# A gated linear recurrence beside dense products: emission of the recurrence's steps moved by one or two products

## The chip, the cores and the metric

The kernel runs on one core of one Trainium2 chip. The metric is the device time of one execution in microseconds (us); the time before is 2263.52 us, the median of three runs (2262.01 to 2264.18). The core has a matrix engine (PE, whose weight loads PEld run beside it), a vector engine (DVE), a scalar engine (ACT), GpSimd (POOL) and SyncE (SP), which starts the DMAs. Each engine works through its own queue of instructions; semaphores tie the queues together.

## The reference

Two transformer blocks follow each other on 1024 tokens of width 1024, all in float32. The change touches the first mixer of the first block only:

```
proj = h @ w_in                       # 1024 x 4096: q, f, i, g
k    = (1 - lb) * sigmoid(-f);  decay = lb + (1 - lb) * sigmoid(f)
q    = silu(q) * 128 ** -0.5
S_t  = diag(decay_t) S_{t-1} + k_t v_t^T ;  o_t = S_t^T q_t     # 8 heads of 128
out  = (rms_norm per head of o) * out_norm * silu(g) @ w_out
```

With one layer the lower bound lb is 0. After this mixer come a squared-ReLU MLP, a second mixer (a short convolution beside a retention) and a second MLP, which the change leaves as they are.

## The kernel before, in words

Every large product is made of three float32r matmuls (high by high, high by low, low by high part), which the helper `mm3` (L210) issues. This text calls one such triple over 512 columns "a product". `unit` (L216) makes one 128x512 tile of a projection from 8 products; `unit_b` (L230) makes the values' tiles from triples of 256 columns, half a product each. Between them a small planner runs: `at(delay, fn)` (L144) files a function under a slot number, and `tick` (L147) runs all functions filed under the present slot, in the order in which they were filed, and raises the number. `unit` ticks after its fourth product and at its end, `unit_b` after each 8 triples of 256 columns, so there are four products' worth of columns between two ticks. What a function issues in a tick goes to the end of each engine's queue, and the queue is worked through in that order.

In `run`, the first mixer goes through 8 heads. For each head a `unit` pair makes f (4 ticks) and a pair makes q (4 ticks); before each even head but the first, `unit_b` makes the values of two heads (8 ticks). After q's first half (L792 to L795) DVE multiplies the tile by the row norm (L609), ACT takes the sigmoid (L794) and DVE forms the query tile qf (L795); the same follows for the second half. Then `hgrn_scan` (L354) files the recurrence of the head under later slots, by the table `SCAN_AT` (L37), counted from the slot of the call:

- `diag` at 0: 64 small matmuls (L367), and DVE copies them under a mask (L372)
- `level0` at 0: nine DVE instructions (queries and totals, L386 to L434)
- `level1` at 2: 64 small matmuls (`scores`, L413); on DVE the queries forward (L401 to L403), new queries (L389, L390, behind copies by ACT at L388), the keys (L442, L443), the masked copies (L420) and totals (L432 to L434)
- `level2` at 5: `scores` again (L413), then DVE L402, L403, L442, L443, L420
- `level(16)`, `level(32)`, `level(64)` at 7, 8, 10: small matmuls (L367 for 16 tokens, L485 for 32 and 64), a copy by DVE (L476) or ACT (L489), then three DVE instructions: totals (L492), keys kr (L493), queries qf (L494)
- `krt` at 12: seven transposes of kr on PE (L539)
- `states` at 15: L554 on PE, L560 and L562 on DVE; `outs` at 16: L574 and L576 on PE, squares on ACT (L585), sums on DVE (L586); `scale` at 21 (L593); `final` at 24 (L603)

Two heads take 24 slots: 8 for the values, 4 each for f, q, f and q. If the even head of a pair calls at slot 16, the odd one calls at slot 24, 8 slots later. So two heads' steps meet in some slots. Slot 24 holds the previous odd head's `final`, the even head's `level(32)`, the odd head's `diag` and `level0`. Slot 26 holds the even head's `level(64)`, then the odd head's `level1`; slot 28 the even head's `krt`. Slot 16 holds `final` of the head two before, `outs` of the one before, and `diag` and `level0` of the head itself. After head 7 the gates' units take the place of the values; their tiles are handled by `gate` (L612), which files a DVE product (L620) for the next tick and another (L624) for the one after it.

Of the kernel before, what the change touches and what calls it, by code (L numbers as in the profile page):

```python
# [17 lines left out]
MUL, ADD, SUB, MAX = ALU.mult, ALU.add, ALU.subtract, ALU.max  # L18
# [3 lines left out]
T = 1024  # L22
D = 1024
KT = 8
HALF = 512
# [9 lines left out]


SCAN_AT = (0, 0, 2, 5, 7, 8, 10, 12, 15, 16, 21, 24)  # L37
RETENTION_AT = (2, 4, 5, 5, 13, 14)
CONV_NORM_AT = (2, 4, 5)
CONV_SPLIT_AT = (50, 52, 54, 56)  # L40
# [57 lines left out]
class Kernel:  # L98
    def __init__(self, tc, ctx, x, w, consts, masks, tab, out):
        self.tc, self.nc = tc, tc.nc  # L100
        self.low = self.nc.vector
        self.x_dram, self.w_dram, self.c_dram = x, w, consts
        self.m_dram, self.tab_dram, self.out_dram = masks, tab, out
        cp = ctx.enter_context(tc.tile_pool(name="consts", bufs=1))
        self.cp = cp
        self.sm = ctx.enter_context(tc.tile_pool(name="small", bufs=2))
        self.tp = ctx.enter_context(tc.tile_pool(name="tmp", bufs=N_TMP))
        self.slots = Slots(ctx.enter_context(tc.tile_pool(name="slots", bufs=1)), N_SLOTS)
        self.acc = ctx.enter_context(tc.tile_pool(name="acc", bufs=4, space=bass.MemoryType.PSUM))
        self.ps2 = ctx.enter_context(tc.tile_pool(name="ps2", bufs=4, space=bass.MemoryType.PSUM))  # L110
        self.slot = 0
        self.plan = defaultdict(list)
        self.n = 0
        self.stage = {}
        self.split = {}
        self.next_load = 0
        self.next_split = 0
        self.next_use = 0
        self.look = N_LOOK
        self.apart = 0  # L120
        self.limit = FIRST_MLP
        self.dram = ctx.enter_context(tc.tile_pool(name="dram", bufs=1, space=bass.MemoryType.DRAM))
# [22 lines left out]
        self.plan[self.slot + delay].append(fn)  # L145

    def tick(self):  # L147
        while self.slot in self.plan:
            for fn in self.plan.pop(self.slot):
                fn()  # L150
        self.slot += 1

    def drain(self):
        while self.plan:
            self.tick()


# [52 lines left out]
    def mm3(self, ps, ah, al, bh, bl, start, stop):  # L210
        mm = self.nc.tensor.matmul
        mm(ps, lhsT=ah, rhs=bh, start=start, stop=False)  # L212
        mm(ps, lhsT=ah, rhs=bl, start=False, stop=False)  # L213
        mm(ps, lhsT=al, rhs=bh, start=False, stop=stop)  # L214

    def unit(self, w, src, half):  # L216

# [136 lines left out]
    def hgrn_scan(self, h, qf, kr, f, v):  # L354
# [6 lines left out]
        st = {"off": 0}  # L361
# [8 lines left out]
        def diag():  # L370
            ps = small(self.bank(), lambda t: qf[:, t:t + 32], 32)
            ve.copy_predicated(ac, self.masks[:, M_DIAG:M_N], ps)  # L372
            st["tots"] = S.get("tots")

# [15 lines left out]
        def advance(i, half, tot):  # L392
            b = B4[i]
            n = HALF // (4 * b)
            r = st.pop((i, half))
            rv = r[:, :768].rearrange("p (v n b) -> p v n b", v=6, b=b)
            g = slice(half * n, (half + 1) * n)
            qv = qf.rearrange("p (n j b) -> p j n b", j=4, b=b)[:, :, g]
            d0 = tot.rearrange("p (n j) -> p j n", j=4)[:, 0:1, g, None].to_broadcast([P, 2, n, b])
            if i == 0:  # L400
                ve.tensor_tensor(qv[:, 0], qv[:, 0], d0[:, 0], op=MUL)  # L401
            ve.tensor_tensor(qv[:, 1], rv[:, 0], d0[:, 0], op=MUL)  # L402
            ve.tensor_tensor(qv[:, 2:4], rv[:, 3::2], d0, op=MUL)  # L403
            S.put(r)

        def scores(i):
            b = B4[i]
# [37 lines left out]


        def level0():
            for half in range(2):
                queries(0, half, f)
            st["d1"], st["e0"] = totals(0, f)  # L450

        def level1():
            keep = scores(0)
            for half in range(2):
                advance(0, half, f)
                queries(1, half, st["d1"])
            keys(0, f, st["e0"])
            keep()
            st["tot"], st["e1"] = totals(1, st["d1"])
            S.put(f)  # L460

        def level2():
            keep = scores(1)
            for half in range(2):
                advance(1, half, st["d1"])
            keys(1, st["d1"], st["e1"])
            keep()

        def level(b):
            n = T // (2 * b)  # L470
            ps = self.bank()
            qv = qf.rearrange("p (n two b) -> p n two b", two=2, b=b)
            kv = kr.rearrange("p (n two b) -> p n two b", two=2, b=b)
            if b == 16:
                pv = small(ps, lambda t: qv[:, t // (2 * b):(t + 32) // (2 * b), 1, :], 16)
                ve.copy_predicated(ac.rearrange("p (n two b) -> p n two b", two=2, b=b)[:, :, 1, :],  # L476
                                   self.masks[:, M_16:M_DIAG].rearrange("p (n b) -> p n b", b=b),
                                   pv.rearrange("p (n b) -> p n b", b=b))
            else:
                av = a.rearrange("p (n two b) -> p n two b", two=2, b=b)  # L480
                nb = P // (2 * b)
                for c in range(NCH):
                    for j in range(nb):
                        r = slice(2 * b * j, 2 * b * j + b)
                        mm(ps[r, c * b:(c + 1) * b], lhsT=kv[:, c * nb + j, 0, :], rhs=qv[:, c * nb + j, 1, :],  # L485
                           start=True, stop=True)
                for j in range(nb):
                    r = slice(2 * b * j, 2 * b * j + b)
                    nc.scalar.copy(av[r, j::nb, 1, :], ps[r, :NCH * b].rearrange("p (n b) -> p n b", b=b))  # L489
            tv = st["tot"].rearrange("p (n two) -> p n two", two=2)  # L490
            new = st["tots"][:, st["off"]:st["off"] + n]
            ve.tensor_tensor(new, tv[:, :, 0], tv[:, :, 1], op=MUL)  # L492
            nc.vector.tensor_tensor(kv[:, :, 0, :], kv[:, :, 0, :], tv[:, :, 1:2].to_broadcast([P, n, b]), op=MUL)  # L493
            nc.vector.tensor_tensor(qv[:, :, 1, :], qv[:, :, 1, :], tv[:, :, 0:1].to_broadcast([P, n, b]), op=MUL)  # L494
            st["off"] += n
            st["tot"] = new
            if b == 16:
                for r in range(0, P, 32):
                    nc.scalar.copy(a3[r:r + 32, :, r:r + 32], ac[r:r + 32].rearrange("p (c t) -> p c t", t=32))
# [22 lines left out]
            S.put(st["os"])  # L522

        t = SCAN_AT
        for i, fn in enumerate((diag, level0, level1, level2)):
            self.at(t[i], fn)
        for i in range(3):
            self.at(t[4 + i], lambda i=i: level(16 << i))
        for i, fn in enumerate((krt, states, outs, scale, final)):
            self.at(t[7 + i], fn)  # L530

    def transpose7(self, src, dst, scale):

# [108 lines left out]
    def run(self):  # L642
# [126 lines left out]
        for h in range(8):  # L769
            if h % 2 == 0 and h:  # L770
                vs = [S.get("v"), S.get("v")]
                ws = self.use(2)
                for p in range(4):
                    ps = self.unit_b(ws, u, p)
                    self.values(ps, p, vs, zs)
                self.done(ws)
            f, kr, qf = S.get("f"), S.get("kr"), S.get("qf")
            ws = self.use()
            for half in range(2):
                tk = slice(half * HALF, (half + 1) * HALF)  # L780
                ps = self.unit(ws[0], u, half)
                z = self.times_rb(ps, half)
                nc.scalar.activation(f[:, tk], z, AF.Sigmoid)
                nc.scalar.activation(kr[:, tk], z, AF.Sigmoid, scale=-1.0)
                nc.scalar.activation(f[:, tk], f[:, tk], AF.Identity, scale=self.omlb[:, h:h + 1],
                                     bias=self.lb[:, h:h + 1])
            self.done(ws)
            ws = self.use()
            for half in range(2):
                tk = slice(half * HALF, (half + 1) * HALF)  # L790
                ps = self.unit(ws[0], u, half)
                z = self.times_rb(ps, half)  # L792
                sg = self.tmp()
                nc.scalar.activation(sg, z, AF.Sigmoid)  # L794
                nc.vector.scalar_tensor_tensor(qf[:, tk], z, self.c1[:, h:h + 1], sg, op0=MUL, op1=MUL)  # L795
                if half == 1:
                    self.hgrn_scan(h, qf, kr, f, vs[h % 2])
            self.done(ws)

# [969 lines left out]
```

## Time and profile before

| | |
|---|---|
| time, median of 3 runs | 2263.52 us (2262.01 to 2264.18) |
| profiled execution, its own time | 2263.14 us |
| span of its instructions | 2261.4 us |
| PE busy | 2233.7 us, 99% of the span |
| DVE busy | 1775.9 us, 79% |
| ACT busy | 856.0 us, 38% |
| mean granted clock of PE | 0.997 |
| PE busy from 100 to 200, 200 to 300, 300 to 400 us (first mixer) | 97.39, 97.39, 97.27 us |
| PE busy in each 100 us from 600 to 1100 us | 100.00 us |

Times are microseconds from the start of the span. "Busy" is the time in which an engine works on an instruction; a number in brackets behind a row, as [1.01 <-DVE qf L795], is the idle time of the engine just before that instruction and the instruction on the other engine that ended it. [...]

### The profile page before, as it was taken

Reading aid. Unit: us, or ns where it says so; the run is one execution under the profiler, and the core shown is the slowest. Engines: PE = TensorE matmul, PEld = TensorE weight load, DVE = VectorE, ACT = ScalarE, POOL = GpSimd, SP = SyncE. Lnnn points to the kernel's source line nnn. Section 1 sums busy time; section 2 is a strip of 40 time slices with the busy share of each in tenths; the row PEclk is TensorE's granted clock in tenths of the full one; section 3 lists DMA queues with packets and bytes.
Section 4 is the critical chain, followed back from the end, with each engine's and each line's share of the span. In section 5 each row is a group of like instructions: output and inputs, shape, how many; then the busy total and the mean of one; then the engine's idle time right before and its main releaser. Section 6 shows DMA issues by size and latency. Waiting matters only on the chain.

```text
span 2261.4 us, 32861 instructions
## 1 busy us (share of the span) xinstructions
PE 2233.7 (99%) x13102; PEld 1883.5 (83%) x13102; DVE 1775.9 (79%) x2674; ACT 856.0 (38%) x1259; POOL 347.0 (15%) x340
## 2 busy tenths in 40 slices
PE   8999999999999999999999999999999999999998
PEld 7888897888888888888889888888888888888887
DVE  6757668736988888989996556885798888889896
ACT  6333333434433335433344232224533333634322
POOL 0020101101111111222210011000111111222223
PEclk9999999999999999999999999999999999999999
DMA  5001011122344448544514101113334445744442
GB/s 182 30 29 39 20 39 39 47 85 112 128 175 157 153 167 291 167 140 160 194 38 187 38 29 46 39 38 118 125 135 177 149 151 212 263 142 155 153 158 75
DMA packets 82521, 270.30 MB, mean 120 GB/s; under 512 B 9152, under 2 KB 11712, under 8 KB 82368
## 3 DMA queue, kind: packets, MB, share of 16 engines
q1 hardware_dynamic: 81792, 267.67, 33.8%
q8 instruction: 103, 1.69, 0.3%
q10 hardware_dynamic: 576, 0.52, 0.1%
q14 instruction: 50, 0.41, 0.1%
HBM read 190.57 MB, written 77.59 MB: 119 GB/s over the span
## 4 chain that ended last, share of the span: by engine, by line
PE 89%; DVE 8%; ACT 2%; issue 1%; DMA 0%; SPq 0%; DVEq 0%; ACTq 0%
PE acc L212 21%; PE acc L213 21%; PE acc L214 21%; PE ps L212 7%; PE ps L213 7%; PE ps L214 7%; PE ps L574 1%; PE ps L576 1%; PE ps L554 1%; DVE ac L420 1%; DVE lo L178 1%; DVE tmp L609 1%; DVE r L389 0%; PE ps L485 0%; PE ps L539 0%
## 5 line engine op out<-in xcount | busy, mean ns | idle before, releaser
L212 PE MATMUL acc<-hi,hi 128*128 128x512 f32 (+1 forms) x824 | 315.1, 382 | 0.5 <-ACT acc L1255 0.4
L214 PE MATMUL acc<-hi,lo 128*128 128x512 f32 (+1 forms) x824 | 313.8, 381 | 0.0
L213 PE MATMUL acc<-lo,hi 128*128 128x512 f32 (+1 forms) x824 | 313.8, 381 | 0.0
L212 PE MATMUL acc<-uh,hi 128*128 128x512 f32 x768 | 305.6, 398 | 0.0
L214 PE MATMUL acc<-uh,lo 128*128 128x512 f32 x768 | 299.4, 390 | 0.0
L213 PE MATMUL acc<-ul,hi 128*128 128x512 f32 x768 | 299.1, 389 | 0.0
L212 PE MATMUL ps<-hi,hi 128*128 128x512 f32 x712 | 277.2, 389 | 0.0
L214 PE MATMUL ps<-hi,lo 128*128 128x512 f32 x712 | 277.0, 389 | 0.0
L213 PE MATMUL ps<-lo,hi 128*128 128x512 f32 x712 | 277.0, 389 | 0.0
L1198 ACT ACTIVATE hq<-hq 128x512 f32<-128x512 f32 x128 | 81.0, 634 | 333.3 <-DVE hq L1197 267.3
L212 PEld LDWEIGHTS acc<-hi,hi 128*128 128x128 f32 x824 | 154.9, 188 | 31.4 <-ACT acc L1255 1.1
L214 PEld LDWEIGHTS acc<-hi,lo 128*128 128x128 f32 x824 | 154.9, 188 | 29.8
L213 PEld LDWEIGHTS acc<-lo,hi 128*128 128x128 f32 x824 | 154.9, 188 | 29.7 <-issue 0.2
L214 PEld LDWEIGHTS acc<-uh,lo 128*128 128x128 f32 x768 | 144.1, 188 | 30.8
L212 PEld LDWEIGHTS acc<-uh,hi 128*128 128x128 f32 x768 | 144.2, 188 | 30.0 <-ACT v L638 0.2
L213 PEld LDWEIGHTS acc<-ul,hi 128*128 128x128 f32 x768 | 144.3, 188 | 28.7 <-issue 0.5
L214 PEld LDWEIGHTS ps<-hi,lo 128*128 128x128 f32 x712 | 133.6, 188 | 28.0
L212 PEld LDWEIGHTS ps<-hi,hi 128*128 128x128 f32 x712 | 133.6, 188 | 27.7
L213 PEld LDWEIGHTS ps<-lo,hi 128*128 128x128 f32 x712 | 133.7, 188 | 27.6
L189 ACT CAST hi<-h 128x1024 fp32r<-128x1024 f32 x96 | 100.4, 1055 | 134.0 <-DVE lo L190 76.5
L190 DVE TENSOR_TENSOR lo<-h,hi 128x1024 fp32r<-128x1024 f32 x96 | 122.1, 1280 | 6.3 <-ACT hi L189 6.3
L178 DVE TENSOR_TENSOR lo<-w,hi 128x1024 fp32r<-128x1024 f32 x74 | 89.8, 1219 | 28.4 <-ACT hi L175 28.3
(278 smaller groups left out, 4644.3 us busy)
## 6 DMA issues: line engine op xcount, KB each, us to landing
w<-in_w SPq DMA_DIRECT2D x202, 512.0 KB, 4.5
hf<-f SPq DMA_DIRECT2D x28, 512.0 KB, 2.6
hfull<-hq SPq DMA_DIRECT2D x28, 512.0 KB, 3.5
hg<-g SPq DMA_DIRECT2D x28, 512.0 KB, 4.1
h<-hfull SPq DMA_DIRECT2D x28, 512.0 KB, 3.6
h<-hf SPq DMA_DIRECT2D x28, 512.0 KB, 4.4
h<-hg SPq DMA_DIRECT2D x28, 512.0 KB, 3.4
xs<-x SPq DMA_DIRECT2D x16, 512.0 KB, 2.8
```

Of the source, the lines that this page charges most:

```text
L178: self.low.tensor_tensor(lo, st, hi.bitcast(F32), op=SUB)
L189: self.nc.scalar.copy(hi, src)
L190: self.low.tensor_tensor(lo, src, hi.bitcast(F32), op=SUB)
L212: mm(ps, lhsT=ah, rhs=bh, start=start, stop=False)
L213: mm(ps, lhsT=ah, rhs=bl, start=False, stop=False)
L214: mm(ps, lhsT=al, rhs=bh, start=False, stop=stop)
L420: ve.copy_predicated(av[:, j:], mask[:, v0:v1], pm[:, v0:v1])
L554: nc.tensor.matmul(ps[:, c * P:(c + 1) * P], lhsT=kt[:, t], rhs=v[:, t], start=True, stop=True)
L574: nc.tensor.matmul(o, lhsT=a3[:, i, :], rhs=v[:, t], start=True, stop=(i == 0))
L576: nc.tensor.matmul(o, lhsT=qx[:, t], rhs=s[:, t], start=False, stop=True)
L609: self.nc.vector.tensor_tensor(z, ps, self.rb[:, half * HALF:(half + 1) * HALF], op=MUL)
L1198: nc.scalar.activation(t, t, AF.Square)
```

## The change

No instruction of the computation is added or taken out; the order in which they stand in the engines' queues changes. `mm3` counts the products issued (`work`), and a new function `defer(n, fn)` puts a function on a list that is looked through after each triple: it runs once n products more have been issued, at the next tick at the latest. A table beside `SCAN_AT` says which step is deferred within its slot, and by how many products: `diag` by 2, `level0`, `level(32)`, `level(64)` and `outs` by 1, the others by 0. In `level2` the queries are moved forward first, and the rest (scores, keys, copies) is deferred by 2. In `level(16)` the small matmuls stay at the tick, and the masked copy and the three DVE instructions behind it are deferred by 1. The product L795 of q's first half is filed for the next tick; before that of the second half, everything on the list is issued first.

```diff
+SCAN_LATE = (2, 1, 0, 0, 0, 1, 1, 0, 0, 1, 0, 0)
     def tick(self):
+        self.flush()
         while self.slot in self.plan:
...
+    def defer(self, n, fn):
+        self.late.append((self.work + n, fn))
+        self.late.sort(key=lambda e: e[0])
+    def flush(self, upto=float("inf")):
+        while self.late and self.late[0][0] <= upto:
+            self.late.pop(0)[1]()
...
         mm(ps, lhsT=al, rhs=bh, start=False, stop=stop)
+        self.work += bh.shape[-1] / HALF
+        self.flush(self.work)
...
         def level2():
-            keep = scores(1)
             for half in range(2):
                 advance(1, half, st["d1"])
-            keys(1, st["d1"], st["e1"])
-            keep()
+            def rest():
+                keep = scores(1)
+                for half in range(2):
+                    S.put(st.pop((1, half)))
+                keys(1, st["d1"], st["e1"])
+                keep()
+            self.defer(2, rest)
...
             if b == 16:
                 pv = small(ps, lambda t: qv[:, t // (2 * b):(t + 32) // (2 * b), 1, :], 16)
-                ve.copy_predicated(ac.rearrange("p (n two b) -> p n two b", two=2, b=b)[:, :, 1, :],
-                                   self.masks[:, M_16:M_DIAG].rearrange("p (n b) -> p n b", b=b),
-                                   pv.rearrange("p (n b) -> p n b", b=b))
+                self.defer(1, lambda: (ve.copy_predicated(
+                    ac.rearrange("p (n two b) -> p n two b", two=2, b=b)[:, :, 1, :],
+                    self.masks[:, M_16:M_DIAG].rearrange("p (n b) -> p n b", b=b),
+                    pv.rearrange("p (n b) -> p n b", b=b)), next_level(b, qv, kv)))
             else:
...
+                next_level(b, qv, kv)
+        def next_level(b, qv, kv):
+            n = T // (2 * b)
             tv = st["tot"].rearrange("p (n two) -> p n two", two=2)
             new = st["tots"][:, st["off"]:st["off"] + n]
             ve.tensor_tensor(new, tv[:, :, 0], tv[:, :, 1], op=MUL)
...
+        steps = (diag, level0, level1, level2, *(lambda i=i: level(16 << i) for i in range(3)),
+                 krt, states, outs, scale, final)
+        for i, (fn, n) in enumerate(zip(steps, SCAN_LATE)):
+            self.at(t[i], (lambda fn=fn, n=n: self.defer(n, fn)) if n else fn)
...
-                nc.vector.scalar_tensor_tensor(qf[:, tk], z, self.c1[:, h:h + 1], sg, op0=MUL, op1=MUL)
-                if half == 1:
+                def product(tk=tk, z=z, sg=sg, qf=qf, h=h):
+                    nc.vector.scalar_tensor_tensor(qf[:, tk], z, self.c1[:, h:h + 1], sg, op0=MUL, op1=MUL)
+                if half == 0:
+                    self.at(0, product)
+                else:
+                    self.flush()
+                    product()
                     self.hgrn_scan(h, qf, kr, f, vs[h % 2])
```

Of the tiles, `tots` is taken in `level0` in place of `diag`, and the tiles r are given back in `level1` and in the deferred part of `level2`.

## Rows read from the trace of the kernel before

**Rows 1.** From the profile's page: busy time of PE over the span (time, share, instructions), and the chain of work that ended last, its shares by engine. From the table by stretches, one stretch in which PE only makes products: length, PE busy time (and matmuls), PEld, DVE, ACT and POOL busy time, granted clock, DMA share, GB/s.

```profile
PE 2233.7 (99%) x13102; PEld 1883.5 (83%) x13102; DVE 1775.9 (79%) x2674; ACT 856.0 (38%) x1259; POOL 347.0 (15%) x340
...
PE 89%; DVE 8%; ACT 2%; issue 1%; DMA 0%; SPq 0%; DVEq 0%; ACTq 0%
...
700.00:800.00 100.00, 100.00 (x443) 82.81 (x442) 84.01 (x113) 33.94 (x48) 15.87 (x11) 1.00 0.41 149
```

**Rows 2.** What PE waited for from 60 to 470 us, the stretch of the recurrences: total us, times, longest us. These are all the rows of that answer.

```profile
PE ps L485 <- DVE qf L494: 4.1, 5, 1.0
PE ps L367 <- DVE qf L795: 4.0, 4, 1.0
PE ps L413 <- DVE kr L443: 1.8, 3, 0.6
PE ps L576 <- DVE s L560: 0.6, 1, 0.6
```

**Rows 3.** PE in order of time around the meeting of heads 2 and 3, the second of the four pairs: start, length, line, tile and count, and in brackets the idle time before. L413 is `level2` of head 2, L485 with 128x32 `level(32)` of head 2, L367 `diag` of head 3, L485 with 128x64 `level(64)` of head 2, L413 after it `level1` of head 3, L539 `krt` of head 2.

```profile
170.64 0.89 PE L413 MATMUL ps<-r,kr 128*32 128x48 f32 x64 [0.61 <-DVE kr L443]
...
182.86 0.64 PE L485 MATMUL ps<-qf,kr 128*32 128x32 f32 x29 [0.90 <-DVE qf L494]
...
184.82 0.46 PE L367 MATMUL ps<-qf,kr 128*32 128x32 f32 x32 [1.01 <-DVE qf L795]
...
192.64 1.15 PE L485 MATMUL ps<-qf,kr 128*64 128x64 f32 x16
193.71 0.89 PE L413 MATMUL ps<-r,kr 128*32 128x48 f32 x64
...
200.39 0.93 PE L539 MATMUL ps<-cs,kr 128*128 128x128 f32 x7
```

**Rows 4.** DVE in order of time in the same pair, up to the meeting: the sums behind `outs`, the keys of `level1` of head 2, the query products of both halves, the queries of `level(16)`, and the second half's eviction (L609).

```profile
155.16 0.69 DVE L586 TENSOR_REDUCE ss<-tmp 128x4 f32<-128x512 f32 x1 [1.10 <-ACT tmp L585]
...
169.89 0.60 DVE L443 TENSOR_TENSOR kr<-kr,f 128x256 f32<-128x256 f32 x1
...
180.46 0.75 DVE L795 SCALAR_TENSOR_TENSOR qf<-tmp,c,tmp 128x512 f32<-128x512 f32 x1 [0.70 <-ACT tmp L794]
...
182.03 0.69 DVE L494 TENSOR_TENSOR qf<-qf,tots 128x512 f32<-128x512 f32 x1
182.63 0.69 DVE L609 TENSOR_TENSOR tmp<-acc,rb 128x512 f32<-128x512 f32 x1
184.01 0.75 DVE L795 SCALAR_TENSOR_TENSOR qf<-tmp,c,tmp 128x512 f32<-128x512 f32 x1 [0.70 <-ACT tmp L794]
```

**Rows 5.** DVE in order of time behind the meeting: the masked copy of `diag`, the first instruction of `level0`, a weight split (L178), the keys of `level(64)` of head 2, the first instruction of `level1` of head 3, and the first behind the last one of `level1`.

```profile
185.97 0.44 DVE L372 COPY_PREDICATED ac<-masks,ps 128x256 f32<-128x256 uint8 x1
186.31 0.86 DVE L386 TENSOR_TENSOR r<-qf,f 128x384 f32<-128x384 f32 x1
...
191.88 1.22 DVE L178 TENSOR_TENSOR lo<-w,hi 128x1024 fp32r<-128x1024 f32 x1
193.02 0.16 DVE L492 TENSOR_TENSOR tots<-tots 128x8 f32<-128x8 f32 x1
193.82 0.69 DVE L493 TENSOR_TENSOR kr<-kr,tots 128x512 f32<-128x512 f32 x1 [0.64 <-PE ps L485]
...
195.03 0.38 DVE L401 TENSOR_TENSOR qf<-qf,f 128x128 f32<-128x128 f32 x1
...
204.00 0.28 DVE L402 TENSOR_TENSOR qf<-r,tots 128x128 f32<-128x128 f32 x1
```

**Rows 6.** PE in the other pairs, in order of time: `level(32)` and `krt` of the first pair; `level2` and `krt` of the third; `level2` and `krt` of the fourth; and `level(32)` of head 7.

```profile
88.82 0.64 PE L485 MATMUL ps<-qf,kr 128*32 128x32 f32 x29 [0.60 <-DVE qf L494]
...
104.86 0.93 PE L539 MATMUL ps<-cs,kr 128*128 128x128 f32 x7
...
266.17 0.89 PE L413 MATMUL ps<-r,kr 128*32 128x48 f32 x64 [0.61 <-DVE kr L443]
...
294.44 0.93 PE L539 MATMUL ps<-cs,kr 128*128 128x128 f32 x7
...
360.24 0.89 PE L413 MATMUL ps<-r,kr 128*32 128x48 f32 x64 [0.62 <-DVE kr L443]
...
387.98 0.93 PE L539 MATMUL ps<-cs,kr 128*128 128x128 f32 x7
...
408.24 0.70 PE L485 MATMUL ps<-qf,kr 128*32 128x32 f32 x32 [0.67 <-DVE qf L494]
```

**Rows 7.** The granted clock, from the table by stretches for PE alone: length, PE busy time (matmuls), granted clock, DMA share, GB/s. The first two stretches are in the second pair, the third at the same place in the third pair.

```profile
184.00:186.00 2.00, 1.18 (x37) 0.91 0.03 8
186.00:188.00 2.00, 2.00 (x11) 0.50 0.00 0
...
280.00:282.00 2.00, 1.65 (x42) 1.00 0.00 0
```

**Rows 8.** Three rows for durations. Two triples of the values apart on PE (start to start of the first matmul of two neighbouring triples of 256 columns), and the gate's DVE product behind `level1` of head 7.

```profile
190.03 0.28 PE L212 MATMUL acc<-hi,uh 128*128 128x256 f32 x1
...
190.39 0.28 PE L212 MATMUL acc<-hi,uh 128*128 128x256 f32 x1
...
393.39 0.68 DVE L620 TENSOR_TENSOR tmp<-tmp,on 128x512 f32<-128x512 f32 x1
```

More of the change, by code (lines that the diff above doesn't have):

```diff
@@ L112, in __init__ @@
         self.plan = defaultdict(list)
+        self.late = []
+        self.work = 0.0
         self.n = 0
@@ L151, in tick @@
         self.slot += 1
+    def defer(self, n, fn):
[4 more added lines that the diff above has]
+            self.late.pop(0)[1]()
     def drain(self):
-        while self.plan:
+        while self.plan or self.late:
             self.tick()
@@ L372, in diag @@
             ve.copy_predicated(ac, self.masks[:, M_DIAG:M_N], ps)
-            st["tots"] = S.get("tots")
         def queries(i, half, tot):
@@ L394, in advance @@
             n = HALF // (4 * b)
-            r = st.pop((i, half))
+            r = st[i, half]
             rv = r[:, :768].rearrange("p (v n b) -> p v n b", v=6, b=b)
@@ L403, in advance @@
             ve.tensor_tensor(qv[:, 2:4], rv[:, 3::2], d0, op=MUL)
-            S.put(r)
         def scores(i):
@@ L447, in level0 @@
         def level0():
+            st["tots"] = S.get("tots")
             for half in range(2):
@@ L455, in level1 @@
                 advance(0, half, f)
+                S.put(st.pop((0, half)))
                 queries(1, half, st["d1"])
@@ L524, in hgrn_scan @@
         t = SCAN_AT
[L525 to L530, printed above, removed]
+        steps = (diag, level0, level1, level2, *(lambda i=i: level(16 << i) for i in range(3)),
+                 krt, states, outs, scale, final)
+        for i, (fn, n) in enumerate(zip(steps, SCAN_LATE)):
+            self.at(t[i], (lambda fn=fn, n=n: self.defer(n, fn)) if n else fn)
     def transpose7(self, src, dst, scale):
```

## The prediction

> **What bounds the kernel now.** I read the page first: PE is busy for 99% of the span, and PE holds 89% of the chain that ended last [rows 1]. From 600 us on PE makes products without a gap, so the first mixer is where idle time can be won. There I asked what PE waits for: four kinds of wait, 4.1 + 4.0 + 1.8 + 0.6 = 10.5 us, and that is all [rows 2]. Then I laid PE and DVE side by side around one meeting of two heads. The waits sit where DVE runs behind: at `level2` of the even head (0.61), at its `level(32)` (0.90) and at `diag` of the odd head (1.01), 2.52 us in a full pair [rows 3]. DVE is late for two reasons: it stands idle for 0.70 us before each product L795, for ACT's sigmoid, and before that it waited at L586 for the squares behind `outs`, with `level0` queued behind [rows 4].
>
> A second price is PE's clock. [...] The pairs show the cost: from L413 to L413 it is 266.17 - 170.64 = 95.53 us with the fall and 360.24 - 266.17 = 94.07 without [rows 3, 6], so one fall costs 1.46 us.
>
> **The change part by part.** No instruction is added; only places in queues move. Moved steps issue PE, DVE and ACT instructions, and `outs` some small POOL ones that go with it; none issues a DMA, so SP's queue is as before. My unit is four products between ticks: a product takes 3 x 100/443 = 0.68 us [rows 1], and two value triples take 2 x 0.36 = 0.72 [rows 8]. From the start of a DVE update to the start of the PE step that needs it I take 182.86 - 182.03 = 0.83 us [rows 3, 4].
>
> *Queries' product.* The first half's L795 a tick later has its sigmoid done; the second half's now follows the level of 16 tokens, four DVE instructions that cover the sigmoid. Both waits of 0.70 go: 1.40 us less of DVE's queue ahead of slot 24.
>
> *`outs` behind one product.* PE starts it 0.68 us later, and the sums L586 and all behind them follow, `level0` too, which only changes places with the copy of `diag`. That is +0.68 on DVE, except in the first pair, which has no `outs` there. Where the deferral of `level0` itself costs anything, DVE has other work, so I put it at 0.
>
> *`level2` behind two products.* PE asks for the keys 1.36 us later than before; they come 0.68 later and were 0.61 late: 1.36 - 0.68 - 0.61 = 0.07 to spare. The wait of 0.61 goes, barely.
>
> *`level(32)`.* PE was ready at 182.86 - 0.90 = 181.96; now 0.61 earlier and two triples later, 182.07. The queries L494 start at 182.03 + 0.68 (outs) - 0.70 (first sigmoid) + 0.60 (eviction L609 now ahead of them) = 182.61, so PE goes at 183.44: a wait of 1.37 [rows 3, 4]. *`diag`:* L795 starts at 184.01 + 0.68 - 1.40 = 183.29; PE arrives after two more triples, near 184.7, and doesn't wait. A full pair thus goes from 2.52 to 1.37, 1.15 saved. In the first pair both waits go (0.60 + 1.01 = 1.61); at head 7's end 0.59 + 0.67 = 1.26 are at stake [rows 2, 6].
>
> *`level(64)` behind one product.* This is the expensive part. Slot 26 holds `level(64)` of the even head and `level1` of the odd one. Before, the former came first: L492 to L494 stood ahead of L401 on DVE, and on PE L485 ahead of L413 [rows 3, 5]. Now `level1`, which is not deferred, runs in the tick, and `level(64)` follows it. So the even head's keys L493 stand behind all of `level1`, 204.00 - 195.03 = 8.97 us of DVE [rows 5]. Two ticks later `krt` transposes these keys on PE, and behind it on PE's queue stand the products. Before, there were 200.39 - 193.82 = 6.57 us between the keys and `krt`, so nobody waited; that cover is gone.
>
> Second pair: DVE comes to `level1` at 193.02 + 0.68 - 1.40 = 192.30; + 8.97 = 201.27; + 0.1 for L492; the keys start at 201.37 and `krt` at 202.2. Before: 200.39. So PE, though 1.15 us ahead at its arrival (199.24), leaves `krt` 1.8 us later than before. Third pair: 95.53 us later, 297.7 against 294.44: +3.3 (no fall of the clock in the old one). Fourth pair, 360.24 - 170.64 = 189.60 later than the second: 391.8, plus the gate's eviction L609 and product L620 in the same queue, 0.60 each: 393.0 against 387.98, +5.0 [rows 3, 6, 8]; that delay then swallows the 1.26 of head 7, so +3.7. First pair: PE starts L485 at 88.22 + 0.72 = 88.94; DVE's keys behind it at about 89.5; L493 and L494 1.2, `level0` 5.57, L372 0.34, L178 1.14, `level1` 8.97, L492 0.1: keys at 106.8, `krt` at 107.65 against 104.86, +2.8 [rows 5, 6]. Sum: 2.8 + 1.8 + 3.3 + 3.7 = 11.6 us slower. The waits at `krt` would be 4.4, 3.0 to 4.4, 4.4 and 6.2 us long. Behind them DVE has caught up (it only waits for PE until the next pair), so nothing is won back.
>
> *The clock behind such waits.* No row shows a wait of 4 to 6 us in the middle of dense work. Bounds from rows: 0, as after the 1.9 us of waits in the third pair, or a full fall, 1.46, at each of four places, 5.8 in all; twice that if a fall should last twice as long. Since waits of 1.9 us within 4 us already brought a fall in one of several cases [rows 7], I take it in three places of four, 4.4 us. [...]
>
> **Sum.** The profiled execution took 2263.1 us for a span of 2261.4 and lies 0.4 below the median. 2263.1 + 11.6 + 4.4 = 2279.1; I predict 2279.
>
> **The rivals.**
>
> *A. `krt` is not held, faster.* Place: the update of `level(64)` on DVE. If it got ahead of `level1` after all (instructions put in another order than issued, or a deferral that runs earlier than I read), `krt` never waits and only the savings are left: 1.61 + 3 x 1.15 + 1.26 = 6.3 and the one fall of 1.46: 2255.3. It decides from the point where the keys start before about 197 us in the second pair, 0.83 and a little before PE's arrival. For it: `krt` had 6.57 us to spare. Against: in rows 4 DVE waits for 1.10 us before L586 although `level0` behind it needs nothing of it; order is kept. 12%.
>
> *B. `krt` waits, but the clock holds.* 2274.7. For it: the third pair. Against: the waits are more than twice as long. 18%.
>
> *C. Longer falls.* Where a wait of 4 to 6 us costs two falls' worth at each place, 2263.1 + 11.6 + 4 x 2 x 1.46 = 2286.4. Nothing in the trace shows a fall that long inside dense work. 10%.
>
> *D. The waits at `krt` are short,* because `level1` runs faster without the neighbours of before (its waits for ACT's copies shrink): at half of 11.6 and no fall the time is 2268.9; if they vanish but the other waits stay, about 2263, no change. 10%.
>
> **How the numbers follow.** The forecast has 50% (2275.5 to 2283). A measurement of this kernel can tell about 0.2%, 4.5 us, from no change. Faster: A, 12%. Same: 8%, most of D. Slower: forecast, B, C and the rest of D, 80%. The range 2267 to 2286 takes in the forecast, B and the most of C and of D; outside lie A, the lower end of D and the upper of C.
>
> **What would show it.** Waits of PE in the profile after: a new row, PE L539 for DVE kr L493, four times and 15 to 20 us in total, the longest in the fourth pair; L367 for L795 and L413 for L443 gone; L485 for L494 three times near 1.4. On DVE L493 with 128x8 totals before it would stand behind L434 of the next head, and L795 without idle time before it at slots 22 and 23. The granted clock would read 0.50 for some microseconds behind two or more of the `krt`. If `krt` has no wait in the profile, the prediction is wrong by its main term; if it has and the clock is at 1.00, it is wrong by its second.

## The result and the profile after

The changed kernel takes 2293.81 us (median of 4 runs, 2293.06 to 2294.4) against 2262.77 for the kernel before: ratio 1.0142, 95% interval 1.0129 to 1.0155. It is 31 us slower; I had predicted 2279, so the direction was right and the size about half. The profiled execution took 2294.4 us for a span of 2292.6.

Line numbers shift: in the changed kernel the small matmuls of `diag` and of the level of 16 tokens are L383 (L367 before), those of levels 32 and 64 L508 (L485), `scores` L427 (L413), the keys of `level1` and `level2` L456 and L457 (L442, L443), the updates behind a level L519 to L521 (L492 to L494), the transposes L564 (L539), the query product L822 (L795), the queries forward and totals L416 to L418 and L446 to L448 (L401 to L403, L432 to L434), the eviction L634 (L609), the weight split L192 (L178).

The page's busy time of the engines, to hold against [rows 1]:

```profile
PE 2245.1 (98%) x13102; PEld 1892.6 (83%) x13102; DVE 1775.5 (77%) x2674; ACT 855.7 (37%) x1259; POOL 345.5 (15%) x340
```

PE runs the same 13102 matmuls, yet it is busy 2245.1 - 2233.7 = 11.4 us longer: that is PE at a lower clock (a mean granted clock of 0.991 against 0.997), as the stretches below show. What PE waited for in the recurrences' stretch (total us, times, longest), all rows of the answer, to hold against [rows 2]:

```profile
PE ps L564 <- DVE kr L520: 18.2, 4, 6.3
PE ps L383 <- DVE kr L457: 12.3, 4, 3.9
```

All four old waits (10.5 us) are gone, and two new ones stand there, 30.5 us. So 20.0 us of idle time and 11.4 us of slower work make 31.4; the two spans differ by 31.2.

The second pair on PE, in order of time, against [rows 3]:

```profile
176.12 0.89 PE L427 MATMUL ps<-r,kr 128*32 128x48 f32 x64
...
185.18 1.06 PE L383 MATMUL ps<-qf,kr 128*32 128x16 f32 x64 [3.87 <-DVE kr L457]
...
193.12 0.70 PE L508 MATMUL ps<-qf,kr 128*32 128x32 f32 x32
...
211.97 1.73 PE L564 MATMUL ps<-cs,kr 128*128 128x128 f32 x7 [4.02 <-DVE kr L520]
```

And DVE in the same stretch, against [rows 4, 5]:

```profile
182.27 1.23 DVE L192 TENSOR_TENSOR lo<-w,hi 128x1024 fp32r<-128x1024 f32 x1 [0.59 <-ACT hi L189]
183.41 0.68 DVE L634 TENSOR_TENSOR tmp<-acc,rb 128x512 f32<-128x512 f32 x1
184.02 0.68 DVE L456 TENSOR_TENSOR kr<-kr,tmp 128x512 f32<-128x512 f32 x1
184.61 0.42 DVE L457 TENSOR_TENSOR kr<-kr,tots 128x256 f32<-128x256 f32 x1
...
185.82 0.74 DVE L822 SCALAR_TENSOR_TENSOR qf<-tmp,c,tmp 128x512 f32<-128x512 f32 x1
...
193.87 0.69 DVE L520 TENSOR_TENSOR kr<-kr,tots 128x512 f32<-128x512 f32 x1 [4.45 <-PE ps L508]
...
202.13 0.40 DVE L416 TENSOR_TENSOR qf<-qf,f 128x128 f32<-128x128 f32 x1
...
211.06 0.16 DVE L519 TENSOR_TENSOR tots<-tots 128x8 f32<-128x8 f32 x1
211.14 0.69 DVE L520 TENSOR_TENSOR kr<-kr,tots 128x512 f32<-128x512 f32 x1
```

Two places are to be read here. At 211.06 the even head's update of the level of 64 tokens stands behind all of the odd head's `level1` (202.13 to 211.1), and the transposes at 211.97 start 0.83 us after the keys: the wait I had predicted. At 182.27 to 184.6 the keys of `level2` (L456, L457) stand behind a weight split (L192) and an eviction (L634) that they used to stand ahead of, and the level of 16 tokens, which reads these keys, waits for 3.87 us. That one I had not seen.

The granted clock (1.00 is full speed), by stretches for PE alone (length, busy time and matmuls, clock, DMA share, GB/s): around the 0.8 us wait at L383 in the first pair, then behind the seven long waits.

```profile
83.00:86.00 3.00, 2.39 (x78) 1.00 0.77 257
...
107.00:112.00 5.00, 5.00 (x24) 0.50 0.34 107
185.00:190.00 5.00, 4.82 (x82) 0.50 0.01 5
...
212.00:215.00 3.00, 3.00 (x15) 0.50 0.00 0
...
290.00:295.00 5.00, 5.00 (x33) 0.66 0.01 3
...
314.00:318.00 4.00, 3.34 (x17) 0.57 0.00 0
...
393.00:396.00 3.00, 3.00 (x9) 0.50 0.00 0
...
417.00:422.00 5.00, 2.96 (x11) 0.50 0.06 10
```

The clock stays at 1.00 around the short wait and falls behind each of the seven waits of 3.8 us or more: at 107, 185 and 417 it reads 0.50 for the whole of 5 us, at 212 and 393 for 3 us, and at 290 and 314 the means are 0.66 and 0.57. Behind the wait at 185 matmuls of 256 columns start 0.21 us apart (from 186.97 to 191.03), where those of [rows 8] start 0.12 apart.

### The profile page after: what moved, and what is told of

Its sections match the earlier page's. It is cut to its first block, busy times and chain, and to the rows that moved or that the text cites. A ratio compares the mean times of both kernels' runs of the same rounds, so it can differ in the third digit from the quotient of the medians.

```text
span 2292.6 us, 32856 instructions
## 1 busy us (share of the span) xinstructions
PE 2245.1 (98%) x13102; PEld 1892.6 (83%) x13102; DVE 1775.5 (77%) x2674; ACT 855.7 (37%) x1259; POOL 345.5 (15%) x340
## 4 chain that ended last, share of the span: by engine, by line
PE 88%; DVE 9%; ACT 2%; issue 1%; DMA 0%; SPq 0%; DVEq 0%; ACTq 0%
PE acc L226 20%; PE acc L228 20%; PE acc L227 20%; PE ps L226 7%; PE ps L228 7%; PE ps L227 7%; PE ps L599 1%; PE ps L601 1%; PE ps L579 1%; DVE r L404 1%; DVE ac L434 1%; DVE lo L192 1%; PE ps L564 1%; DVE r L401 1%; DVE r L405 0%
## 5 line engine op out<-in xcount | busy, mean ns | idle before, releaser
L192 DVE TENSOR_TENSOR lo<-w,hi 128x1024 fp32r<-128x1024 f32 x74 | 89.8, 1220 | 31.7 <-ACT hi L189 31.6
```

Of the source, the lines that this page charges most:

```text
L192: self.low.tensor_tensor(lo, st, hi.bitcast(F32), op=SUB)
```

## The experiments

Times are medians; "before" is the kernel before on the same chip, 2261.5 us in the first two sets and 2261.9 in the last. It was 2262.8 in the set of the changed kernel, so a difference between an experiment and the changed kernel is known to about 1.3 us.

The line numbers move with the edits. In the rows below L559 and L552 are the transposes, L427 and L426 `scores`, L503 and L498 the level of 32 tokens (L504 that of 64), L383 the level of 16 tokens, L380 `diag`, L457 and L456 the second keys' instruction of `level1` and `level2`, L515 and L506 the keys and L516, L517 and L507 the queries behind a level, L808 and L818 the query product, L607 the sums behind `outs`.

**One entry undone: the level of 64 tokens.**

```diff
-SCAN_LATE = (2, 1, 0, 0, 0, 1, 1, 0, 0, 1, 0, 0)
+SCAN_LATE = (2, 1, 0, 0, 0, 1, 0, 0, 0, 1, 0, 0)
```

> The changed kernel with one entry of the table undone: the level of 64 tokens is no longer deferred, so its keys stand ahead of the other head's level1 again. Theory 1 (two separate queue orders, each with falls of the clock behind it): PE's wait at the transposes (18.2 us, four times) goes and with it the falls behind these four places, about 7 us; the wait at the level of 16 tokens (3 x 3.8 and 0.8) stays with its three falls. 2293.8 - 18.2 - 7 = about 2268. Theory 2 (DVE is simply too late in this stretch, and a wait that is removed turns up elsewhere): less than half of it, 2281 or more, with a new or longer wait at another line.

Measured: 2270.52 us, ratio to before 1.0039 (1.0024 to 1.0054). The only wait left in the stretch:

```profile
PE ps L383 <- DVE kr L457: 15.0, 5, 3.9
```

The wait at the transposes is gone, and 23.3 us with it (22.0 if each kernel is taken against the kernel before of its own set): 18.2 of waiting, less the 2.7 that the other wait gained at head 7, where PE had been late enough before, and some 7 of clock (the mean granted clock of the profiled execution is 0.995 against 0.991). Theory 2 asked for 2281 or more; it falls for this term.

**level2 as it was, the rest changed.**

```diff
         def level2():
+            keep = scores(1)
             for half in range(2):
                 advance(1, half, st["d1"])
-            def rest():
-                keep = scores(1)
-                for half in range(2):
-                    S.put(st.pop((1, half)))
-                keys(1, st["d1"], st["e1"])
-                keep()
-            self.defer(2, rest)
+                S.put(st.pop((1, half)))
+            keys(1, st["d1"], st["e1"])
+            keep()
```

> The changed kernel with level2 as it was (scores, queries, keys and copies all at the tick), all else changed. Theory 1: PE's wait at the level of 16 tokens for level2's keys (12.3 us) goes with its three falls (about 5 us); the wait at level2's scores for level1's keys comes back, 0.61 + 0.68 = 1.3 us three times; the wait at the transposes stays near 4, 4, 4 and 6 us. 2293.8 - 12.3 - 5 + 3.9 = about 2280. Theory 2 (the wait moves on): about 2290, with the wait at the transposes grown by what the other lost.

Measured: 2283.5 us, ratio 1.0094 (1.0078 to 1.0111). The waits:

```profile
PE ps L559 <- DVE kr L515: 18.2, 4, 6.3
PE ps L427 <- DVE kr L457: 3.8, 3, 1.3
PE ps L503 <- DVE qf L516: 2.5, 3, 0.9
```

The wait at the level of 16 tokens (12.3) is gone, the one at the scores is back with the 1.3 us I had worked out, that at the transposes (now L559) is as long as it was to a tenth. Neither of the two new waits makes the other in these pairs. A small wait at the level of 32 tokens (L503) came, 2.5 us, which I had not put in.

**Both undone.** The two edits above together.

> Both undone: the level of 64 tokens not deferred and level2 as it was; the rest of the change stays (query products, level of 16 tokens, diag, level0, level of 32 tokens and outs deferred). Theory 1: what is left is the gain I had worked out: waits near 4 us (level2's scores, 1.3 three times) in place of 10.5, and no fall: 2262.8 - 6.5 - 1.5 = about 2255, faster than before. Theory 2: DVE is too late anyway: 2262 or more, with waits of PE of 10 us or more.

Measured: 2258.63 us, ratio 0.9988 (0.9978 to 0.9997): a little faster than before. Waits:

```profile
PE ps L503 <- DVE qf L516: 4.3, 4, 1.9
PE ps L427 <- DVE kr L457: 3.8, 3, 1.3
PE ps L383 <- DVE kr L457: 0.3, 1, 0.3
```

8.4 us of waits against the 4 expected; the excess is at the level of 32 tokens. The time fell by 2.9 us where 8 were expected. Against this kernel the two harmful parts are priced: `level2` 2270.5 - 2258.6 = 11.9 us, the level of 64 tokens 2283.5 - 2258.6 = 24.9; together 36.8. The changed kernel lies 2293.8 - 2258.6 = 35.2 above (33.9 if each is taken against the kernel before of its own set). They add up to within 3 us; the 2.7 us of waiting at head 7 count in the first price alone, since in the changed kernel PE is late there anyway.

**Filling the wait at the transposes with work.** The result of the added matmuls is not used; no output depends on it.

```diff
         def krt():
+            if h % 2 == 0:
+                pad = self.accb()
+                for i in range(9 if h == 6 else 6):
+                    for j in range(3):
+                        mm(pad, lhsT=self.u[i % KT][0][:, j * P:(j + 1) * P], rhs=self.u[i % KT][0][:, :HALF],
+                           start=i + j == 0, stop=False)
+                mm(pad, lhsT=self.u[0][0][:, :P], rhs=self.u[0][0][:, :HALF], start=False, stop=True)
             st["krt"] = t = S.get("krt")
...
+        self.u = u
```

> The changed kernel, and ahead of each even head's transposes of the keys PE makes matmuls whose result is not used: 19 of 128x512 (about 4.3 us) in the first three pairs, 28 (about 6.3 us) in the fourth, about as long as its waits there. It tells the wait from the clock. If the clock falls because PE idles, the falls behind these four places go and the time is that of the changed kernel less about 7 us: 2287, although PE does more work. If the clock has nothing to do with these waits, or the falls cost nothing, the time stays at 2294 or grows by what the fillers last beyond the waits.

Measured: 2289.72 us, ratio to before 1.0122 (1.0107 to 1.0137); 4.1 us less than the changed kernel (2.8 if each is taken against the kernel before of its own set), with 85 matmuls more. PE by stretches around the first pair's transposes, then behind the wait at the level of 16 tokens in the third pair:

```profile
104.00:108.00 4.00, 4.00 (x24) 1.00 0.02 4
108.00:112.00 4.00, 4.00 (x36) 1.00 0.41 131
...
284.00:290.00 6.00, 5.10 (x83) 0.50 0.01 3
```

The clock stays at 1.00 where it read 0.50 in the changed kernel (107 to 112); in the second pair it reads 1.00 from 210 to 218, where it had read 0.50 from 212 to 215. The fillers last about 1 us longer than the waits did (an estimate from 0.226 us a matmul [rows 1]: 3 x 4.3 + 6.3 = 19.2 against 18.2), so the clock gave back 4 to 5 us net. This was the run that told the clock from the wait: with the waits at the transposes filled there was no fall there in the first two pairs, and the time fell although PE did more work, so these falls went with PE's idle time and cost time of their own. The 4 to 5 us are the least that the four falls cost: the falls behind the other wait stayed, and in two of three pairs they lasted longer than in the changed kernel (284 to 290 at 0.50 throughout, where 290 to 295 read 0.66; the mean granted clock is 0.993 against 0.991). The first experiment, in which the other falls lasted as long in all as in the changed kernel, puts the four at some 7 us.

**`outs` not deferred either.** Both undone, and the tenth entry of the table 0.

```diff
-SCAN_LATE = (2, 1, 0, 0, 0, 1, 0, 0, 0, 1, 0, 0)
+SCAN_LATE = (2, 1, 0, 0, 0, 1, 0, 0, 0, 0, 0, 0)
```

> As the kernel with both undone, and outs not deferred either. My term for outs was 0.68 us on DVE for everything behind the sums. By it PE's wait at level2's scores falls from 1.3 to 0.6, three times: 2 us less than with both undone, 2256.6 against 2258.6. If outs does not set when DVE gets to level0, waits and time stay: 2258.6.

Measured: 2256.77 us, ratio 0.9978 (0.9968 to 0.9987). The rows that matter:

```profile
PE ps L503 <- DVE qf L516: 3.6, 4, 1.2
PE ps L427 <- DVE kr L457: 1.8, 3, 0.6
```

The wait at the scores falls from 1.3 to 0.6 as the 0.68 us asked for, the time by 1.9 as expected. The deferral of `outs` delays DVE, since `level0` stands behind the sums.

**The query products alone.** As the last one, with all entries of the table 0. The copies and updates of the level of 16 tokens stay deferred by one product; the second half's query product follows them.

```diff
-SCAN_LATE = (2, 1, 0, 0, 0, 1, 0, 0, 0, 0, 0, 0)
+SCAN_LATE = (0, 0, 0, 0, 0, 0, 0, 0, 0, 0, 0, 0)
```

> The query products alone: all entries of the table 0 and level2 as it was; only the first half's product a tick later, and the second half's behind the masked copy and the three updates of the level of 16 tokens. By my working DVE has 1.4 us less ahead of slot 24: the wait at diag (1.0, four times) goes, that at level 32 falls by 0.1 to about 0.8, those at level2's scores stay at 0.6: about 6.5 us of waits in place of 10.5, 2261.5 - 4 - about 1 for the clock = 2256.5. The rival: the two sigmoid waits were covered and DVE is held by something else: 2261.

Measured: 2258.99 us, ratio 0.9987 (0.9977 to 0.9996). The waits that matter:

```profile
PE ps L503 <- DVE qf L516: 7.6, 5, 1.9
PE ps L427 <- DVE kr L457: 1.8, 3, 0.6
```

The wait at `diag` (4.0) is gone as expected. The one at the level of 32 tokens, which should have fallen a little, rose from 4.1 to 7.6: with `level2` at the tick nothing stands between the first half's eviction and its product, and DVE still idles there for 0.70 us (at 178.38 in the second pair); the version after the next shows the same row below. So the second half's eviction, now ahead of the queries, adds its 0.60 in full: 0.90 + 0.60 = 1.50, and the second pair's wait is 1.49. The time is 2.5 us above the 2256.5 expected and 2.5 below the kernel before.

**The level of 64 tokens alone,** on the kernel before.

```diff
-            self.at(t[4 + i], lambda i=i: level(16 << i))
+            self.at(t[4 + i], (lambda: self.defer(1, lambda: level(64))) if i == 2 else lambda i=i: level(16 << i))
```

with `defer`, `flush` and the count in `mm3` as in the change.

> The kernel before with one thing alone: the level of 64 tokens deferred by one product. Theory 1: the keys stand behind 9 us of level1 whatever else is done: waits at the transposes of 4.0, 2.5 to 4, 4.0 and 5.7 us, and falls of the clock behind them, about 7 us in all: 2261.5 + 16.5 + 7 = about 2285, with the old waits of 10.5 us still there. Theory 2 (the wait needs the rest of the change, which moved DVE's work): 2265 or less.

Measured: 2281.85 us, ratio 1.0086 (1.0071 to 1.0101). Waits:

```profile
PE ps L552 <- DVE kr L506: 15.2, 4, 5.9
PE ps L380 <- DVE qf L808: 4.0, 4, 1.0
PE ps L498 <- DVE qf L507: 3.4, 4, 1.0
PE ps L426 <- DVE kr L456: 1.8, 3, 0.6
```

This one edit makes the old kernel 20 us slower, 3 less than expected; the waits at the transposes are 3.57, 3.59, 2.18 and 5.89 us in the order of the pairs, the third shorter than the 4.0 expected. Theory 2, which asked for 2265 or less, falls: the queue order does it without any help.

**level0 ahead of the sums, a version meant to beat both.**

```diff
-SCAN_LATE = (2, 1, 0, 0, 0, 1, 0, 0, 0, 1, 0, 0)
+SCAN_LATE = (2, 0, 0, 0, 0, 1, 0, 0, 0, 1, 0, 0)
...
-                self.defer(1, lambda: (ve.copy_predicated(
+                run = (lambda n, fn: fn()) if h % 2 else self.defer
+                run(1, lambda: (ve.copy_predicated(
```

> A version meant to beat both. As with both undone, but level0 runs at the tick while outs stays one product later, so that DVE does the nine instructions of level0 before the sums behind outs and does not idle there; and the copies of the level of 16 tokens are deferred for even heads only. Theory 1 (PE's waits come from DVE standing still ahead of level0 and of the query products): DVE is about 3 us earlier at level2's keys, no wait of PE of 0.5 us or more is left, and no fall: 2261.5 - 10.5 - 1.5 = about 2250. Theory 2 (DVE's total work bounds this stretch): 2257 or more, with waits at other lines.

Measured: 2250.25 us, ratio to before 0.9946 (0.9931 to 0.9961). All its waits in the stretch, PE by stretches (length, then PE, PEld, DVE, ACT, POOL, clock, DMA), and DVE behind the query product of head 2:

```profile
PE ps L504 <- DVE qf L517: 1.1, 1, 1.1
```

```profile
100.00:200.00 100.00, 100.00 (x1240) 89.20 (x1239) 73.73 (x159) 38.51 (x79) 9.51 (x24) 1.00 0.10 33
200.00:300.00 100.00, 100.00 (x1236) 89.00 (x1235) 69.09 (x150) 34.84 (x68) 9.51 (x24) 1.00 0.10 33
300.00:400.00 100.00, 100.00 (x1101) 83.63 (x1100) 75.40 (x155) 40.95 (x73) 9.51 (x24) 1.00 0.12 38
```

```profile
148.87 0.75 DVE L818 SCALAR_TENSOR_TENSOR qf<-tmp,c,tmp 128x512 f32<-128x512 f32 x1 [0.70 <-ACT tmp L815]
149.54 0.86 DVE L401 TENSOR_TENSOR r<-qf,f 128x384 f32<-128x384 f32 x1
...
155.16 1.26 DVE L607 TENSOR_REDUCE ss<-tmp 128x4 f32<-128x512 f32 x2
...
175.53 0.75 DVE L818 SCALAR_TENSOR_TENSOR qf<-tmp,c,tmp 128x512 f32<-128x512 f32 x1 [0.70 <-ACT tmp L815]
...
178.30 0.74 DVE L818 SCALAR_TENSOR_TENSOR qf<-tmp,c,tmp 128x512 f32<-128x512 f32 x1
```

`level0` (149.54) follows the query product at once, and the sums at 155.16 find the squares done: the 1.10 us of [rows 4] and the 1.81 us of idle time before the other sum, just ahead of it, are gone. PE is busy for 100.00 of each 100 us where it had been for 97.3, and the clock is at 1.00. One wait is left where none of 0.5 us or more was expected, 1.1 us at head 7's level of 64 tokens. The rows at 175.53 and 178.30 show the two halves: the first still idles for 0.70, the second, behind the level of 16 tokens, does not.

**The rest of level2 by one product in place of two.** The level of 64 tokens undone as in the first experiment.

```diff
-            self.defer(2, rest)
+            self.defer(1, rest)
```

> The level of 64 tokens not deferred, and the rest of level2 deferred by one product in place of two. It asks why the keys of level2 come late. If the order on DVE decides (the rest stands behind the weight split and the first half's eviction either way), nothing changes against two products: the wait at the level of 16 tokens stays at 3.8 three times, 2270.5. If PE's scores are what is late, they come 0.68 us earlier and so do the keys: the wait falls to 3.2, three times 0.7 less, 2268.5 or lower.

Measured: 2272.36 us (2267.71 to 2272.72), ratio 1.0039 (1.0025 to 1.0054). Waits:

```profile
PE ps L383 <- DVE kr L457: 13.1, 5, 3.2
PE ps L427 <- DVE kr L457: 1.8, 3, 0.6
```

Neither expectation holds in full. The wait at the level of 16 tokens fell by 0.7 a time, as the second one said; but the scores now wait 0.6 for `level1`'s keys, and the sum, 14.9, is the 15.0 of two products. PE idles a little earlier for the same total: the keys come when DVE's order lets them, and that is what the first one meant. The time did not fall (ratio 1.0039, as with two products).

## Why the prediction was right or wrong

**The level of 64 tokens, right.** Predicted were waits of 4.4, 3.0 to 4.4, 4.4 and 6.2 us at the transposes; measured 3.95, 4.02, 3.95 and 6.30 in the order of the pairs. The first experiment and the one with this edit alone show that it is this edit, on either kernel. The way there was not the one worked out for the second pair: DVE did not run through to `level1`, it stood idle for 4.45 us (row 193.87), since PE, held at the level of 16 tokens, came late with its matmuls of level 32 (193.12). The size does not hang on this: with `level2` as it was DVE waits no more than 0.2 us there, and the wait is 3.95.

**`level2` behind two products, the step that failed.** I wrote that the wait of 0.61 goes, barely. It did, at the scores; but I had asked only what PE's scores need, not who reads the keys that move with them. The level of 16 tokens does, two ticks later, and before the change its matmuls had just made it. DVE and PE in the second pair of the kernel before:

```profile
176.73 0.42 DVE L443 TENSOR_TENSOR kr<-kr,tots 128x256 f32<-128x256 f32 x1
...
177.94 1.22 DVE L178 TENSOR_TENSOR lo<-w,hi 128x1024 fp32r<-128x1024 f32 x1
179.07 0.68 DVE L609 TENSOR_TENSOR tmp<-acc,rb 128x512 f32<-128x512 f32 x1
```

```profile
177.29 0.72 PE L367 MATMUL ps<-qf,kr 128*32 128x16 f32 x64
```

The matmuls (177.29) start 0.56 us behind the start of the keys (176.73), and PE has not waited; the split and the eviction come after the keys. In the changed kernel these two stand ahead of the keys: the split takes 1.14 us, with 0.59 of waiting for ACT before it, which DVE reaches sooner, and the eviction 0.61. With the 0.68 of `outs` and the 0.61 by which PE comes sooner that is 3.6; measured were 3.8 to 3.9 three times. In the first pair, which has no `outs` there and where the keys had stood 1.81 us ahead of the matmuls, it was 0.8. So the term that I had put at 0.07 us to spare brought 12.3 us of waiting and three falls of the clock; with `level2` as it was the kernel takes 2283.5 us, 9 to 10 less. At the level of 32 tokens I had counted the eviction of the second half; here I left out that of the first.

**The level of 32 tokens.** The wait of 1.37, three times, did not come, because PE, held at the level of 16 tokens, arrived late. With `level2` undone it showed, at 0.8 to 0.9 us a pair in place of 1.37; with head 7 it made 2.5 to 4.3 us in all. The 4.1 us put there thus hid a part of the step that failed: that the sum came no further off was luck.

**The query products.** Of the two waits of 0.70 the second goes; the first goes only where something stands between eviction and product, which in the changed kernel is the deferred part of `level2` (the row at 185.82 has no idle time before it). The gain at `diag` was right, 4.0 us.

**`outs`, right:** 0.68 us on DVE, shown by the fifth experiment.

**The clock, mis-sized.** I took three falls of 1.46 us, 4.4 in all, for the four waits at the transposes. There were seven falls, one behind each wait of 3.8 us or more, three of them behind the wait that I had not seen; and three of the seven read 0.50 for 5 us on end, longer than the one fall I had to go by, that of the second pair in [rows 7], where 188 to 190 reads 0.74 already. PE's busy time grew by 11.4 us on top of the fall that the old kernel already had. The four falls behind the transposes cost some 7 us by the first experiment and at least 4 to 5 by the filler run. The three places of four were my estimate from [rows 7], one place with a fall and one without. In the changed kernel the clock fell behind all seven waits, and in the filler run it read 1.00 where the first two pairs' waits at the transposes were filled; the estimate took too few.

So of the 31 us, 16 were forecast; some 8 of the rest are idle time (12.3 at the level of 16 tokens, less the 4.1 that I had put at the level of 32), some 7 the clock. Rival C, longer falls, was part of it: two of the four places behind the transposes (107 and 417) had one. A, B and D are refuted.

## What to carry to other kernels

When a step is deferred within an in-order queue, list every reader of what it writes, not only the instruction that issues with it, and every instruction that now stands ahead of it: both new waits here are keys that slid behind work that PE was not waiting for. On PE, price a long wait with the slower clock behind it too: here the clock fell behind seven waits of 3.8 to 6.3 us, which cost 11.4 us on top of the waiting. To take waits away, first look where the late engine itself stands still: letting DVE do `level0` while it waited for the squares (with the copies of the level of 16 tokens deferred for even heads only, not tried apart) gave 2258.6 - 2250.3 = 8.4 us. The kernel with both parts undone, on which it stands, lies only 2.9 below the kernel before, and 4.7 once `outs` is not deferred.

## What the runs showed of the hardware

The same wait was not always followed by a fall of the clock. In the kernel with both parts undone and in that with the query products alone PE waits for 1.87 us at the level of 32 tokens of head 7, at nearly the same time of the run. The stretches behind it, the former kernel first:

```profile
405.00:409.00 4.00, 4.00 (x24) 0.57 0.00 0
```

```profile
405.00:410.00 5.00, 5.00 (x23) 1.00 0.00 0
```

In the one the clock reads 0.57 over 4 us, in the other 1.00 over 5. (The former profile is the longest of that kernel's ten runs, 2258.0 to 2260.9 us.) Two waits at the level of 16 tokens of head 7 show the same: behind 2.74 us in the first experiment PE reads 1.00 from 408 to 414, behind 2.71 us in the last experiment 0.50 throughout. The 23 waits of 3.17 to 6.30 us in these profiles were followed by a fall each time; in the run with the level of 64 tokens alone the one of 2.18 us (third pair) was not (1.00 from 303 to 312). No run here settles what decides between these.
